# A two-layer trunk with attention and experts: routing by blocks in turn, four fold steps on VectorE, Q's weights between gate halves

## The chip, the cores and the metric

The kernel runs on one core of a Trainium2 chip. The metric is the device time of one execution in microseconds (us), as the median of several runs. 1216.5 us of the profiled execution are its span, from the first to the last instruction that the profile shows.

The core's engines work beside each other, each through its own list of instructions: TensorE (PE in the profile, PEld for its weight loads), VectorE (DVE), ScalarE (ACT), GpSimd (POOL) and SyncE (SP). SyncE does no arithmetic here; it issues the transfers of weights from the chip's memory, and where an issue has to wait, SyncE stands and everything behind that issue in its list waits too.

## The reference, cut to what matters

The model has two layers. Each has a token-mixing part and a part with experts, both steered by a vector c through six rows of "adaLN" (two shifts, two scales, two gates). There are 256 tokens of 1024 numbers, 32 experts of width 512 in 4 groups, and a token goes to two experts of one group.

```python
for l in range(DEPTH):
    mod = (jax.nn.silu(c) @ w_ada[l] + b_ada[l])[:, None, :]
    sh1, sc1, gt1, sh2, sc2, gt2 = jnp.split(mod, 6, axis=-1)
    h = x * (1 + sc1) + sh1
    proj = h @ w_in[l]
    q, k, v, u, vs = jnp.split(proj, split_at, axis=-1)
    att = diff_attention(rope(q), rope(k), v, lam)
    mix = concat(rms_norm(att), chunk_spatial_gate(u, vs)) @ w_out[l]
    x = layer_norm(DEEPNORM_ALPHA * x + (1 + gt1) * mix, ln1_g[l], ln1_b[l])
    h = x * (1 + sc2) + sh2
    ffn = hier_moe(h, w_grp, b_grp, w_rt, b_rt, w_gate, w_up, w_down)
    x = layer_norm(DEEPNORM_ALPHA * x + (1 + gt2) * ffn, ln2_g[l], ln2_b[l])
```

The parts `rope` and `concat` stand here for a few lines each.

## The kernel before

**The stream of weights.** 467.6 MB of weights are read, each once. Lines 81 to 149 write them into one list, `stream`, in the order in which they are to be loaded: for each layer the adaLN rows of the first part (`s1`), its gate (`g1`), the five sections of w_in (Q, K, V, U, VS), the adaLN rows of the second part (`s2`, eight chunks), w_out, the second gate (`g2`), then the experts. Most chunks are 1 MiB (128 partitions x 2048 numbers). They land in a ring of 18 slots of 1 MiB, which are nine pairs, `w0` to `w8` (the names w_78 to w_86 in the rows of order below). `choose` (line 180) takes one free slot, or for a chunk of 2 MiB a whole free pair. `pump` (line 193) issues the next chunks on SyncE's queue as long as slots are free, and `done` (line 230) gives a slot back once the program has written its last use, and pumps. So a chunk's transfer waits on the chip for the last reader of the chunk that held its slot.

**The experts.** They are sorted by use, so that experts without tokens come last, and are worked on in units (line 52): units 0 to 5 of two experts, with chunks of 1 MiB, and units 6 to 10 of four experts, with whole 2 MiB chunks for the gate, up and down matrices (in units 6 to 9). The order of the last two units is exchanged, so the experts without tokens fall into unit 9, and their loads and matmuls are skipped at run time. For each unit PE gathers tokens (`gps`), runs gate and up (L1297), then down (`dps`, L1387) and adds to `y` (L1306).

**The front of a layer.** `mixing` (line 644) runs the sections, the attention and the output projection `wo`. While PE does that, VectorE folds adaLN weights: `ada_fold` (line 511) is a generator, and each step multiplies 128x512 of a chunk by the matching part of silu(c) and adds it into chunk 0 (L520). A chunk takes four steps. `done` of a chunk stands behind its four steps, so it runs when the generator is asked for the step after them:

```python
        for k in range(4 if (l, part) == (0, "s2") else KD):
            ...
            if k:
                done(("ada", l, part, k))
```

`fold_on(n)` asks n times. `ada_sum` (line 455) then sums chunk 0 over the partitions with four matmuls (L459); chunks that weren't folded take four matmuls each with silu(c) (L464). `ada_cols` (line 497) copies that row with ScalarE, turns it into columns with PE (`adaT`), and copies these with VectorE into `modc`. In layer 0, four of the eight s2 chunks are folded and four are multiplied on PE, in the routing; in layer 1 all eight are folded, and the sum stands in `mixing`.

**The routing** (`routing`, line 1009). It takes X, normalised by `normalise(tci)` for each of the two blocks of 128 tokens (VectorE's statistics, ScalarE's Ln and Exp for the root, then VectorE), makes `hT` (transposes `hTps` on PE, then a scale and shift by `gc` and `bc`, on VectorE and ScalarE or, with `both=False`, on ScalarE alone), takes the logits (`rt`), chooses experts on VectorE, and splits X into three bf16 parts (`part`, `subtract`: a part is cast by ScalarE, PE subtracts it from X in `left`, and so on), which the gathers need. `gate_sum` for g2 (L539) runs in two halves of two chunks, `gate_copy` (L546) copies its row with ScalarE.

The program's order on each engine is the order in which the code calls these steps; there is no planner.

## Time and profile before

| | us |
|---|---|
| median of 3 runs (1219.26 to 1220.87) | 1219.34 |
| the profiled execution | 1218.11 |
| its span | 1216.5 |
| PE busy in the span | 1044.8 |
| VectorE busy | 356.4 |
| ScalarE busy | 157.0 |

The transfers moved 467.60 MB at a mean of 384 GB/s, and the mean granted clock of PE was 0.931 of its full speed. A busy engine alone says little here, since PE and the transfers take turns as the bound: the slices of the span (GB/s) say when the transfers are full, the timeline of SyncE says where an issue stands and for how long, and the timeline of PE, with the idle time ahead of a group in brackets and what ended it, says what PE was waiting for. A timeline row joins like instructions of a line that follow each other; its first number is the start in us from the start of the span, its second how long the group lasts. A matmul of four bytes stands as two records in the trace.

### The profile page before, as it was taken

Reading aid. Unit: us, or ns where it says so; the run is one execution under the profiler, and the core shown is the slowest. Engines: PE = TensorE matmul, PEld = TensorE weight load, DVE = VectorE, ACT = ScalarE, POOL = GpSimd, SP = SyncE. Lnnn points to the kernel's source line nnn. Section 1 sums busy time; section 2 is a strip of 40 time slices with the busy share of each in tenths; the row PEclk is TensorE's granted clock in tenths of the full one; section 3 lists DMA queues with packets and bytes.
Section 4 is the critical chain, followed back from the end, with each engine's and each line's share of the span. In section 5 each row is a group of like instructions: output and inputs, shape, how many; then the busy total and the mean of one; then the engine's idle time right before and its main releaser. Section 6 shows DMA issues by size and latency. Waiting matters only on the chain. (4 is left out here: it accounts for less than half of the span.)

```text
span 1216.5 us, 13939 instructions
## 1 busy us (share of the span) xinstructions
PE 1044.8 (86%) x5351; PEld 422.9 (35%) x5353; DVE 356.4 (29%) x845; ACT 157.0 (13%) x384; POOL 24.1 (2%) x35
## 2 busy tenths in 40 slices
PE   6999998999997767689789998899999868667785
PEld 2465453434342221133135654443434213113221
DVE  1386767112120010031148535621112101003103
ACT  2033132101010010000022323210101001000000
POOL 0200000000000000000000400000000000000000
PEclk8999999999998787799999998989999978788898
DMA  9999989899999999999999953789999999999995
GB/s 320 375 406 352 418 305 370 366 403 421 423 427 427 427 427 427 429 382 421 394 397 401 413 197 139 313 327 406 421 421 429 426 428 429 426 428 428 421 409 197
DMA packets 79963, 467.60 MB, mean 384 GB/s; under 512 B 11053, under 2 KB 11585, under 8 KB 43154
## 3 DMA queue, kind: packets, MB, share of 16 engines
q1 hardware_dynamic: 79522, 465.85, 94.3%
q8 instruction: 45, 0.74, 0.2%
q10 hardware_dynamic: 288, 0.52, 0.1%
q0 software_dynamic: 80, 0.26, 0.1%
q14 instruction: 28, 0.23, 0.0%
HBM read 484.44 MB, written 1.05 MB: 399 GB/s over the span
## 5 line engine op out<-in xcount | busy, mean ns | idle before, releaser
L1387 PE MATMUL dps<-w,eaT_moe 128*32 128x512 f32 (+1 forms) x1024 | 196.7, 668 | 46.4 <-DMA w<-in_w_down_dram 37.7
L1297 PE MATMUL up<-w,XT_moe 128*32 128x512 f32 (+1 forms) x1024 | 184.7, 644 | 38.3 <-DMA w<-in_w_up_dram 38.3
L1297 PE MATMUL gate<-w,XT_moe 128*32 128x512 f32 (+1 forms) x1024 | 184.4, 652 | 33.1 <-DMA w<-in_w_gate_dram 31.0
L1387 PEld LDWEIGHTS dps<-w,eaT_moe 128*32 128x32 f32 (+1 forms) x1024 | 52.5, 131 | 174.6 <-issue 110.8
L1297 PEld LDWEIGHTS gate<-w,XT_moe 128*32 128x32 f32 (+1 forms) x1024 | 53.1, 128 | 157.5 <-issue 107.0
L1353 DVE TENSOR_TENSOR act_moe<-sg_moe,up 128x512 f32<-128x512 f32 x22 | 15.1, 688 | 314.6 <-PE up L1297 285.6
L1297 PEld LDWEIGHTS up<-w,XT_moe 128*32 128x32 f32 (+1 forms) x1024 | 50.9, 127 | 161.8 <-issue 107.4
L1393 DVE TENSOR_TENSOR eo_moe<-dps,gt 128x512 f32<-128x512 f32 x44 | 30.4, 692 | 210.6 <-PE dps L1387 210.6
L650 PE MATMUL sec<-w,hT_front 128*128 128x512 f32 x192 | 84.8, 595 | 2.6 <-DMA w<-in_w_in_dram 2.4
L1306 PE MATMUL y<-eo_moe,wt_moe 128*128 128x512 f32 x176 | 84.9, 607 | 1.6 <-DVE eo_moe L1393 1.6
L1275 PE MATMUL gps<-G_moe,Xp_moe 128*128 128x256 bf16 (+1 forms) x672 | 64.5, 250 | 3.8 <-DVE G_moe L1249 1.5
L1343 ACT ACTIVATE sg_moe<-gate 128x512 f32<-128x512 f32 x22 | 13.1, 597 | 414.9 <-PE gate L1297 414.9
L1281 DVE TENSOR_SCALAR XT_moe<-gps,gc,bc 128x128 f32<-128x128 f32 x88 | 30.6, 405 | 123.0 <-PE gps L1275 123.0
L1275 PEld LDWEIGHTS <-Xp_moe 128*128 128x128 bf16 x672 | 53.1, 98 | 21.9 <-issue 13.0
L650 PEld LDWEIGHTS sec<-w,hT_front 128*128 128x128 f32 x192 | 35.5, 190 | 44.6 <-issue 39.6
L1306 PEld LDWEIGHTS y<-eo_moe,wt_moe 128*128 128x128 f32 x176 | 30.2, 191 | 43.6 <-issue 40.2
L1321 ACT COPY wt_moe<-wtps 128x256 f32<-128x256 f32 x22 | 8.2, 373 | 275.6 <-PE wtps L1319 275.6
L1284 ACT ACTIVATE XT_moe<-gps,bc,gc 128x128 f32<-128x128 f32 x88 | 33.8, 456 | 41.2 <-PE gps L1275 41.2
L520 DVE SCALAR_TENSOR_TENSOR w<-w,csl,w 128x512 f32<-128x512 f32 x56 | 39.1, 768 | 0.0
L659 PE MATMUL sec<-w,hT_front 128*128 128x512 f32 x64 | 30.1, 627 | 1.9 <-DVE hT_front L673 1.9
L842 PE MATMUL u<-hT_front,w 128*128 128x256 f32 x128 | 28.8, 379 | 0.0
L955 PE MATMUL wo<-w,zu_front 128*128 128x512 f32 x64 | 28.1, 592 | 0.0
(283 smaller groups left out, 755.4 us busy)
## 6 DMA issues: line engine op xcount, KB each, us to landing
w<-in_w_gate_dram SPq DMA_DIRECT2D x64, 1024.0 KB, 9.8
w<-in_w_up_dram SPq DMA_DIRECT2D x64, 1024.0 KB, 14.0
w<-in_w_gate_dram SPq DMA_DIRECT2D x32, 2048.0 KB, 24.5
w<-in_w_up_dram SPq DMA_DIRECT2D x32, 2048.0 KB, 22.9
w<-in_w_down_dram SPq DMA_DIRECT2D x32, 2048.0 KB, 23.3
w<-in_w_down_dram SPq DMA_DIRECT2D x56, 1024.0 KB, 13.6
w<-in_w_ada_dram SPq DMA_DIRECT2D x40, 1024.0 KB, 15.2
w<-in_w_in_dram SPq DMA_DIRECT2D x20, 1024.0 KB, 14.8
```

The costliest lines, as they stand in the source:

```text
L520: yield V.scalar_tensor_tensor(acc[:, c], w[:, c], csl[:, k:k + 1], acc[:, c], op0=ALU.mult, op1=ALU.add)
L650: T.matmul(ps, hT[:, k, tci * P:(tci + 1) * P], held["in", l, s, k // 4][:, k % 4, :], start=(k == 0), stop=(k == KD - 1))
L659: T.matmul(ps, hT[:, k, tci * P:(tci + 1) * P], held["in", 0, s, hf][:, k % 4, :], start=(k == 0), stop=(k == KD - 1))
L842: T.matmul(ps[:, 0:NT], held["in", l, U_, k // 4][:, k % 4, g * P:(g + 1) * P], hT[:, k, :], start=(k == 0), stop=(k == KD - 1))
L955: T.matmul(o_ps[tci][h], (cat, zu)[hf][:, kk, tci * P:(tci + 1) * P], w[:, kk, :], start=(hf == 1 and kk == 0), stop=(hf == 0 and kk == 3))
L1275: T.matmul(ps[:, k - kk].rearrange("p j s -> p (j s)"), parts[:, a, tci, k, :], g[:, tci, js[0] * P:(js[-1] + 1) * P], start=(a == 0 and t ...
L1281: V.tensor_scalar(dst, ps[:, k - kk, i, :], gc[:, k:k + 1], bc[:, k:k + 1], op0=ALU.mult, op1=ALU.add)
L1284: S.activation(dst, ps[:, k - kk, i, :], AF.Identity, scale=gc[:, k:k + 1], bias=bc[:, k:k + 1])
L1297: T.matmul(ps[c0:c0 + w], xt[:, k, c0:c0 + w], held[nm, l, place, part][:, k - part[0], :], start=(k == 0), stop=(k == KD - 1))
L1306: T.matmul(y[tci][h], wt[:, tci, :], eo[:, h, :], start=(i == 0), stop=(i == NU - 1))
L1387: T.matmul(dps[h][s0:s0 + w], aT[:, kk, s0:s0 + w], held["down", l, place, part][:, kk - ks[0], c0:c0 + 512], start=(kk == 0), stop=(kk == ...
L1393: V.tensor_tensor(eo[:, h, :], dps[h], gt2[:, h * 512:(h + 1) * 512], op=ALU.mult)
```

## The change

There are four parts.

1. *The folds of layer 0.* s2's chunks 4 to 7 are loaded ahead of w_out instead of behind it, and `ada_fold` folds all eight. In layer 0 the 12 requests in the U section go; 6 come behind the last scores, 6 behind the second block's attention, 4 behind the first residual. The sum of s2 and its columns move from the routing (layer 0) and from the first half of wo (layer 1) to between the last groups of wo.
2. *The routing, in both layers alike.* hT of block 0 is ScalarE's alone; the first half of g2's gate and the first subtraction stand behind it; `normalise(1)` moves from the end of `mixing` to behind that; block 1's transposes and `left` go to other PSUM pools; the parts of block 0 and 1 are cast and subtracted in another order; and the gate's second half and its copy stand ahead of the gathers in both layers (before, in layer 0 the second half stood in `experts`, and the copy in both).
3. *The start of layer 1.* Q's two chunks are loaded between the halves of g1, and the matmuls of Q's first block and the second block's transposes stand ahead of the second gate half. The last statistics of layer 0's second block move from the end of `experts` to behind hT of block 0.
4. `gr` instead of `gsum` is handed from `routing` to `experts` (not shown).

```diff
         if l > 0:
-            add_ada(l, "g1", range(4))
-            add_in(l, [Q_, K_, VS_])
+            add_ada(l, "g1", range(2))
+            add_in(l, [Q_])
+            add_ada(l, "g1", range(2, 4))
+            add_in(l, [K_, VS_])
         add_ada(l, "s2", range(4 if l == 0 else 8))
...
             add_ada(l + 1, "s1", range(4, 8))
+            add_ada(l, "s2", range(4, 8))
         add_out(l)
-        if l == 0:
-            add_ada(l, "s2", range(4, 8))
         add_ada(l, "g2", range(4))
...
         acc = held["ada", l, part, 0][:, 0, :]
-        for k in range(4 if (l, part) == (0, "s2") else KD):
+        for k in range(KD):
             w = held["ada", l, part, k][:, 0, :]
...
             make_hT(lambda k: hT[:, k], gc, bc, 0, early)
-            gate_sum(l, "g1", 2, gsum1)
+            V.bn_stats(sts[1][:, 1, :], y_prev[1][1])
             normalise_psum(1, y_prev[1], sts[1])
             q0 = section(l, Q_, 0)
+            make_hT(lambda k: hT[:, k], gc, bc, 1, early)
+            gate_sum(l, "g1", 2, gsum1)
             gr1 = gate_copy(l, 2, gsum1, fp, "gr")
-            make_hT(lambda k: hT[:, k], gc, bc, 1, early)
         else:
...
         rescale_part(2)
-        fold_on(12)
+        fold_on(12 if l else 0)
         u_part(3)
...
         S.copy(vv[:, 1, :], section(l, V_, 1))
+        if l == 0:
+            fold_on(6)
         ovs = [py.tile([P, 512], F32, tag="s", name=f"att{qc}").rearrange("t (h d) -> t h d", h=H) for qc in range(NTC)]
...
         fold_too(6)
-        asum2 = None
         for tci in range(NTC):
...
                 wo(tci, h, 1)
-            if l > 0 and tci == 0:
-                asum2 = ada_sum(l, "s2", KD)
-            elif l > 0:
-                ada_cols(l, 2, asum2, fp)
             att_T(tci, ats[tci])
             fold_too(8 if tci == 0 else 0)
+            fold_on(0 if tci == 0 else 6)
         ats.clear()
-        asum = None
+        asum = asum2 = None
         for tci in range(NTC):
...
                     ada_cols(l + 1, 0, asum, fp)
+                elif tci == 1 and h == 0:
+                    asum2 = ada_sum(l, "s2", KD)
+                elif tci == 1 and h == 1:
+                    ada_cols(l, 2, asum2, fp)
                 wo(tci, h, 0)
                 residual(tci, h, o_ps[tci][h], gt1, fp)
-            normalise(tci)
+                if tci == 0 and h == 0:
+                    fold_on(4)
+            if tci == 0:
+                normalise(0)
 
...
                 k = slice(4 * h, 4 * h + 4)
-                S.copy(parts[:, a, tci, k], left[tci][h].rearrange("t (k d) -> t k d", k=4))
-
-        def subtract(a, tci):
-            if a == 0:
-                left[tci] = [py.tile([P, 512], F32, tag="s", name=f"left{tci}{h}") for h in range(2)]
-            for h in range(2):
+                S.copy(parts[:, a, tci, k], left[tci, h].rearrange("t (k d) -> t k d", k=4))
+
+        def subtract(a, tci, hs=(0, 1)):
+            for h in hs:
                 k = slice(4 * h, 4 * h + 4)
                 if a == 0:
-                    T.matmul(left[tci][h], ident, X[:, tci, k, :], start=True, stop=False)
-                T.matmul(left[tci][h], minus, parts[:, a, tci, k], start=False, stop=True, skip_group_check=(a > 0))
+                    pool, tag = ((py, "s"), (pm, "m"))[tci]
+                    left[tci, h] = pool.tile([P, 512], F32, tag=tag, name=f"left{tci}{h}")
+                    T.matmul(left[tci, h], ident, X[:, tci, k, :], start=True, stop=False)
+                T.matmul(left[tci, h], minus, parts[:, a, tci, k], start=False, stop=True, skip_group_check=(a > 0))
 
...
         part(0, 0)
-        if l == 0:
-            asum2 = ada_sum(l, "s2", KD // 2)
-            ada_cols(l, 2, asum2, fp, py)
-            gc, bc = affine_cols(l, 1)
-            subtract(0, 0)
-            make_hT(hk, gc, bc, 0, early)
-            part(1, 0)
-        else:
-            gc, bc = affine_cols(l, 1)
-            make_hT(hk, gc, bc, 0, early, both=False)
-            subtract(0, 0)
-            gsum = gate_sum(l, "g2", 5)
-            part(1, 0)
+        gc, bc = affine_cols(l, 1)
+        make_hT(hk, gc, bc, 0, early, both=False)
+        gsum = gate_sum(l, "g2", 5)
+        subtract(0, 0)
+        normalise(1)
         for kk in (0, 4):
-            early[1, kk] = transpose_X(pm, "m", 1, kk)
+            early[1, kk] = transpose_X(py, "s", 1, kk)
         make_hT(hk, gc, bc, 1, early)
         part(0, 1)
+        part(1, 0)
         logits(0)
-        subtract(1, 0)
         logits(1)
...
         subtract(0, 1)
+        subtract(1, 0)
+        part(1, 1)
         part(2, 0)
-        part(1, 1)
-        if l == 0:
-            gsum = gate_sum(l, "g2", 5)
-        else:
-            gate_sum(l, "g2", 5, gsum)
+        gate_sum(l, "g2", 5, gsum)
         subtract(1, 1)
         part(2, 1)
+        gr = gate_copy(l, 5, gsum, fp)
         gl = lg[:, :, 0:NG]
...
         gather(0, (0,))
-        if l == 0:
-            gate_sum(l, "g2", 5, gsum)
-        gr = gate_copy(l, 5, gsum, mp)
         comb, pc = rest(mp)
...
             scatter(NU - 1, tci, (1,))
-            V.bn_stats(st[:, tci, 1, :], y[tci][1])
+            if tci == 0 or l + 1 == L:
+                V.bn_stats(st[:, tci, 1, :], y[tci][1])
         sts = [st[:, tci] for tci in range(NTC)]
```

On PE, from layer 0's last attention matmuls to the routing, the order of before reads as follows (`ada_s` with `onec` is a sum of folded chunks, with `csl` the product with silu(c); `wo` with `cg` are the last four groups of the output projection):

```order
L459 MATMUL ada_s_925<-w_79,onec 32x512 x4
L955 MATMUL wo_882<-w_78,cg_front_773 128x512 x4
L504 MATMUL adaT<-ident,adar_0_front_938 64x128 x8
L955 MATMUL wo_887<-w_79,cg_front_773 128x512 x4
L955 MATMUL wo_907<-w_78,cg_front_773 128x512 x4
L955 MATMUL wo_913<-w_79,cg_front_773 128x512 x4
L629 MATMUL hTps<-ident,X 128x128 x8
L459 MATMUL ada_s_1030<-w_85,onec 32x512 x4
L464 MATMUL ada_s_1030<-w_81,csl 32x512 x4
L464 MATMUL ada_s_1030<-w_82,csl 32x512 x8
L464 MATMUL ada_s_1030<-w_80,csl 32x512 x4
L504 MATMUL adaT<-ident,adar_2_moe_1056 64x128 x8
```

and the order of the changed kernel, at the same place:

```order
L460 MATMUL ada_s_939<-w_79,onec 32x512 x4
L959 MATMUL wo_889<-w_78,cg_front_780 128x512 x4
L505 MATMUL adaT<-ident,adar_0_front_957 64x128 x8
L959 MATMUL wo_894<-w_82,cg_front_780 128x512 x4
L460 MATMUL ada_s_998<-w_85,onec 32x512 x4
L959 MATMUL wo_914<-w_78,cg_front_780 128x512 x4
L505 MATMUL adaT<-ident,adar_2_front_1012 64x128 x8
L959 MATMUL wo_920<-w_82,cg_front_780 128x512 x4
L630 MATMUL hTps<-ident,X 128x128 x8
L437 LDWEIGHTS pick_137
L437 MATMUL gate_g_1071<-rw_136,pick_137 32x512
L437 LDWEIGHTS pick_137
```

The s2 sum (`ada_s_1030` before, `ada_s_998` now) has lost its products with `csl`, and it and its `adaT` have moved ahead of hTps, between wo groups; behind hTps stands the gate's first half.

On SyncE, the loads that follow layer 1's s1 chunks were, before (w_78 to w_86 are the nine pairs; a row with x2 stands for two loads):

```order
L223 DMA w_86<-in_w_out_dram 128x4x512
L223 DMA w_78<-in_w_out_dram 128x4x512 x2
L223 DMA w_79<-in_w_out_dram 128x4x512
L223 DMA w_81<-in_w_ada_dram 128x2048
L223 DMA w_82<-in_w_ada_dram 128x2048 x2
L223 DMA w_80<-in_w_ada_dram 128x2048
L223 DMA w_83<-in_w_ada_dram 128x2x1024 x2
L223 DMA w_80<-in_w_ada_dram 128x2x1024
L223 DMA w_81<-in_w_ada_dram 128x2x1024
```

and are now:

```order
L224 DMA w_78<-in_w_ada_dram 128x2048 x2
L224 DMA w_79<-in_w_ada_dram 128x2048
L224 DMA w_81<-in_w_ada_dram 128x2048
L224 DMA w_82<-in_w_out_dram 128x4x512
L224 DMA w_86<-in_w_out_dram 128x4x512
L224 DMA w_78<-in_w_out_dram 128x4x512
L224 DMA w_82<-in_w_out_dram 128x4x512
L224 DMA w_80<-in_w_ada_dram 128x2x1024
L224 DMA w_83<-in_w_ada_dram 128x2x1024 x2
```

The four 128x2048 loads of w_ada behind the s1 chunks are s2's 4 to 7: they have moved ahead of the four of w_out, into the pairs w_78, w_79 and, the last, w_81.

On PE, at the start of layer 1 (`gate_g` is g1's gate, `sec_0_0` and `sec_0_1` are Q of the two blocks), the order of before:

```order
L436 MATMUL gate_g_3828<-rw_136,pick_137 32x512
L436 LDWEIGHTS pick_137
L436 MATMUL gate_g_3828<-rw_136,pick_137 32x512
L539 MATMUL gate_g_3828<-w_80,csl 32x512 x8
L629 MATMUL hTps<-ident,X 128x128 x8
L539 MATMUL gate_g_3828<-w_84,csl 32x512 x8
L650 MATMUL sec_0_0_3901<-w_86,hT_front_3827 128x512 x8
L629 MATMUL hTps<-ident,X 128x128 x8
L650 MATMUL sec_0_1_3932<-w_86,hT_front_3827 128x512 x8
```

and of the changed kernel:

```order
L437 MATMUL gate_g_3826<-rw_136,pick_137 32x512
L437 LDWEIGHTS pick_137
L437 MATMUL gate_g_3826<-rw_136,pick_137 32x512
L540 MATMUL gate_g_3826<-w_83,csl 32x512 x8
L630 MATMUL hTps<-ident,X 128x128 x8
L651 MATMUL sec_0_0_3890<-w_85,hT_front_3825 128x512 x8
L630 MATMUL hTps<-ident,X 128x128 x8
L540 MATMUL gate_g_3826<-w_84,csl 32x512 x8
L651 MATMUL sec_0_1_3931<-w_85,hT_front_3825 128x512 x8
```

Q of block 0 and the second transposes have moved ahead of the gate's second half.

## Rows read from the trace of the kernel before

**Rows 1.** Page: GB/s moved in 40 slices of 30.4 us.

```profile
GB/s 320 375 406 352 418 305 370 366 403 421 423 427 427 427 427 427 429 382 421 394 397 401 413 197 139 313 327 406 421 421 429 426 428 429 426 428 428 421 409 197
```

**Rows 2.** Windows: span, busy us by engine (x instructions), PEclk, DMA share, GB/s.

```profile
212.00:217.00 5.00, 5.00 (x22) 1.67 (x20) 0.77 (x1) 0.00 (x0) 0.00 (x0) 0.86 0.24 59
250.00:530.00 280.00, 230.38 (x1222) 78.71 (x1222) 39.55 (x74) 15.83 (x38) 0.00 (x0) 0.90 1.01 425
530.00:535.00 5.00, 5.00 (x48) 1.46 (x44) 0.64 (x1) 0.00 (x0) 0.00 (x0) 0.92 0.85 364
535.00:540.00 5.00, 4.85 (x72) 3.15 (x68) 1.46 (x4) 2.21 (x5) 0.00 (x0) 1.00 0.70 242
792.00:799.00 7.00, 6.80 (x22) 2.35 (x24) 2.92 (x4) 0.00 (x0) 0.00 (x0) 0.64 0.16 66
```

**Rows 3.** Timeline of SyncE, layer 0: start, duration, line, operation, count.

```profile
199.67 16.71 SPq L223 DMA_DIRECT2D w<-in_w_gate_dram  x4
...
523.25 13.98 SPq L223 DMA_DIRECT2D w<-in_w_down_dram  x4
```

**Rows 4.** Timeline of PE, layer 0's routing; in brackets idle time before, and releaser.

```profile
158.13 1.06 PE L459 MATMUL ada_s<-w,onec 128*32 128x512 f32 x8
159.01 3.62 PE L464 MATMUL ada_s<-w,csl 128*32 128x512 f32 x32
163.33 1.09 PE L504 MATMUL adaT<-ident,adar_moe 128*64 128x128 f32 x8 [0.71 <-ACT adar_moe L499]
...
172.28 1.93 PE L1029 MATMUL left<-X,ident 128*128 128x512 f32 x2
...
185.68 0.65 PE L1297 MATMUL gate<-w,XT_moe 128*64 128x512 f32 x2 [0.76 <-ACT gr_moe L546]
```

**Rows 5.** Timeline of VectorE, layer 0's attention and output projection.

```profile
122.34 1.02 DVE L800 COPY aT_front<-aTps 128x384 f32<-128x384 f32 x2 [4.12 <-PE aTps L798]
123.28 1.41 DVE L520 SCALAR_TENSOR_TENSOR w<-w,csl,w 128x512 f32<-128x512 f32 x2
...
146.18 0.69 DVE L987 TENSOR_TENSOR res_front<-wo,cg_front 128x512 f32<-128x512 f32 x1 [4.11 <-PE wo L955]
...
150.49 0.69 DVE L987 TENSOR_TENSOR res_front<-wo,cg_front 128x512 f32<-128x512 f32 x1 [1.66 <-PE wo L955]
```

**Rows 6.** SyncE's waits from 520 to 540: total us, times, longest.

```profile
SPq L223 <- PE gate L1297: 12.2, 1, 12.2
```

**Rows 7.** Timeline of PE, unit 9 of layer 0.

```profile
527.20 8.77 PE L1297 MATMUL gate<-w,XT_moe 128*32 128x512 f32 x64
```

**Rows 8.** Timeline of PE, where layer 1 begins.

```profile
614.81 1.09 PE L629 MATMUL hTps<-ident,X 128*128 128x128 f32 x8 [1.59 <-ACT X L621]
615.83 2.23 PE L539 MATMUL gate_g<-w,csl 128*32 128x512 f32 x16
620.45 7.10 PE L650 MATMUL sec<-w,hT_front 128*128 128x512 f32 x16 [2.39 <-DMA w<-in_w_in_dram]
...
628.59 1.95 PE L650 MATMUL sec<-w,hT_front 128*128 128x512 f32 x4 [0.16 <-DVE hT_front L639]
```

**Rows 9.** Timeline of PE, layer 1's routing.

```profile
741.30 1.02 PE L1029 MATMUL left<-X,ident 128*128 128x512 f32 x2
745.88 0.61 PE L1030 MATMUL left<-Xp_moe,minus 128*128 128x512 bf16 x1 [3.55 <-ACT Xp_moe L1017]
...
758.04 1.76 PE L1029 MATMUL left<-X,ident 128*128 128x512 f32 x2
...
767.90 1.51 PE L1297 MATMUL gate<-w,XT_moe 128*64 128x512 f32 x6 [1.38 <-ACT gr_moe L546]
```

**Rows 10.** Timeline of ScalarE, layer 1's routing.

```profile
747.03 2.90 ACT L641 ACTIVATE hT_moe<-hTps,bc,gc 128x128 f32<-128x128 f32 x8 [1.21 <-DVE gc L576]
```

**Rows 11.** Timeline of VectorE, layer 1's routing.

```profile
745.56 0.81 DVE L614 TENSOR_SCALAR X<-X,mv,rs 128x1024 f32<-128x1024 f32 x1
```

**Rows 12.** Timeline of SyncE, unit 9 of layer 1.

```profile
1106.86 14.32 SPq L223 DMA_DIRECT2D w<-in_w_down_dram  x4
```

8 lines of the change are left out of this document (4 added, 4 removed).

## The prediction

> **What bounds the kernel now.** I read the page's slices first. GB/s says where the weights set the time: at 421 and more the transfers are the bound, and where it falls to 305, 352 or 139 they are not [rows 1]. The windows then put times on the falls. Through layer 0's experts from 250 to 530 us DMA is full at 425 GB/s; at 212 to 217 it moves 59 GB/s while PE is busy all the time, and at 792 to 799, the same place of layer 1, 66 GB/s [rows 2]. There SyncE stands before an issue: four loads that it began at 199.67 took 16.71 us to issue [rows 3]. It waits because the ring of 18 slots is full and PE has not yet used up a chunk. So in a front PE's pace sets when a slot comes free, and in the experts DMA sets the pace. The end moves with the last stall of DMA in each layer: a microsecond saved on PE ahead of 247 or of 799 us is a microsecond at the end, and a chunk that the ring can hold less is the time of a chunk at the end. A chunk of 1 MiB (1.049 MB) at 425 GB/s takes 2.5 us and one of 2 MiB 4.9 us.
>
> There is one more hole, at 530 to 540 us, with 364 and then 242 GB/s [rows 2]. It is unit 9 of layer 0 (of 0 to 10), which skips two of its four experts. SyncE issues that unit's first down chunk at 523.25 and can't issue the second until PE is through with gate [rows 3]: it waits 12.2 us for it [rows 6], and gate runs from 527.20 for 8.77 us, to 535.97 [rows 7]. What had been issued lasts until some 534 us (364 of 425 GB/s are 4.3 us of the five from 530).
>
> **Layer 0's routing.** PE's L464 matmuls of s2 go: 3.62 us [rows 4]. The eight matmuls left (1.06 us) and adaT (1.09 us) move between the wo groups, at the same cost to PE, but the wait of 0.71 us for ScalarE's copy ahead of adaT is then hidden by a wo group. The gate row's copy now stands ahead of the gathers on ScalarE, so the 0.76 us before gate(0) go [rows 4]. Together 5.1 us less. Against it stands one new wait. With `both=False` all eight activations of hT(0) are ScalarE's, and normalise(1), which stood ahead of them, now needs ScalarE's Ln and Exp behind them. In layer 1, where the trace has the same eight, they take 2.90 us [rows 10], and X(1) was ready at 745.56 + 0.81 = 746.37 [rows 11]. By my replay of the order (an estimate), gc and bc stand at 743.2, the eight end at 746.1, and Ln, Exp and what follows of the normalisation, 1.9 us, end near 748.0, 1.6 us later than before. PE, which has half of g2's gate and a left pair ahead of X(1)'s transposes now, comes there at 746.5 to 747.2. So PE waits between nothing and all of the 2.9 us; I take 1.2, the middle of 0.8 and 1.5 from the replay. Layer 0: -5.1 + 1.2 = **-3.9 us** (from -5.1 to -2.2).
>
> The 16 matmuls become 16 VectorE steps. Two of them take 1.41 us [rows 5], so 16 cost 11.3 us of VectorE. Twelve stand in front of a wait: six fill the 4.12 us before the aT copy at 122.34, six the 4.11 us before the residual at 146.18 (6 x 0.705 = 4.2 us each) [rows 5]. The last four (2.8 us) stand behind the first residual, ahead of the next at 150.49, which had 1.66 us to wait: it starts 1.1 us later [rows 5]. The later residuals' products come 1 to 2 us later too, since PE has 2.15 us more between its wo groups, so VectorE has caught up by the last. I cost the folds at nothing; without that cover it would be 1.2 us. Their chunks now come ahead of w_out, which pushes w_out by 4 MiB, 9.9 us; as PE's first wo comes after the attention, I expect no wait there.
>
> **The ring.** Folding frees a chunk when its generator is asked for one step more: `done` of chunk k runs on the way to the first step of chunk k + 1, and for chunk 7 only on a 33rd request. Layer 0 now asks 8 + 8 + 6 + 6 + 4 = 32 times. So `done(("ada", 0, "s2", 7))` is never reached, and in the order of SyncE's issues that slot, the second half of w_81, is given to nobody after it: no whole pair of 2 MiB is ever put in w_81 again. From there the ring has 17 slots, and for loads of 2 MiB eight pairs instead of nine. Layer 1 asks for 41, so nothing is lost there a second time. That has three prices. In each layer's front, where DMA runs dry waiting for a slot [rows 2, 3], chunk n waits for the release of n - 17 instead of n - 18: one chunk later, **+2.5 us** in layer 0 and **+2.5 us** in layer 1. If the ring were not what limits, this would be 0 each; if a pair were lost where a pair is needed, 4.9. In unit 9 the chunk that kept DMA busy to the last, until 534 (down 28, 2 MiB, issued at 523.25) finds no pair, and has to wait for gate's end at 535.97 as the ones behind it do. DMA runs dry one 2 MiB chunk earlier and starts again at the same time: **+4.9 us** (0 if something else frees a pair in time; no more, since the restart is set by PE). Elsewhere in the units of four PE is through with a chunk 7 to 10 us after its landing, and eight pairs last 39 us; no hole opens there.
>
> For these three prices the Trainium skill ("DMA: Bandwidth & Descriptors", section Bandwidth) would name another rate: for transfers from HBM the HBM side, some 358 GB/s, is said to bind. By that 1 MiB would take 2.9 us and the three together 11.7 us instead of 9.9. The trace differs with its 425 GB/s.
>
> **Layer 1's front.** Q is 2 MiB nearer, so its chunks land 4.9 us sooner, and Q0 stands ahead of the second gate half. Before, PE had that half at 615.83 and then waited 2.39 us for Q's weights until 620.45 [rows 8]. Now Q0 can start when hT(0) is there: the transposes end at 614.81 + 1.09 = 615.9, the first slice 0.4 later, 616.3. 7.1 us of Q0, the transposes of the second block and the gate half (some 3.0 us together) put Q1 at 626.4, against 628.59 [rows 8]: **-2.2 us** (from -3.0, without the 0.4 and with Q there first, to -1.2, if half of Q's lead is lost on the way). K and U come no later than they did; s2 lands ahead of its folds or about with them.
>
> **Layer 1's routing.** The wait of 3.55 us for the cast of X(0), which stood behind normalise(1) on ScalarE, goes, and the 1.38 us before gate(0) go: -4.9. The same new wait of 1.2 comes: **-3.7 us** (from -4.9 to -2.0) [rows 9].
>
> **The sum.** -3.9 + 2.5 + 4.9 - 2.2 - 3.7 + 2.5 = +0.1 us. On the profiled execution (span 1216.5, with 1.6 us around it 1218.1) that gives 1218.2; the median of the runs shown lies 1.2 above it. I predict 1219.4. Less than 0.2% (2.4 us) from no change can't be told by a measurement of this kernel. The forecast's own range, from the middle parts of the bounds above, is 1217 to 1221.8.
>
> **Rivals.**
> 1. The lost slot costs little: the issues ahead of a stall rearrange, or DMA makes up for unit 9. Then -9.8 remains of the gains alone: 1219.3 - 9.8 = 1209.5. For it: nothing in PE's own work grows. Against it: three stalls with SyncE standing before an issue [rows 2, 3, 6]. Decides: whether DMA restarts at the hole of unit 9 before gate's end. 18%.
> 2. PE's clock. After the wait of 3.55 us two left matmuls take near double: five such pairs stand in the two routings, from 1.93 us at 172.28 [rows 4] to 1.76 at 758.04, against 1.02 for the same pair at 741.30, ahead of the wait [rows 9]; 1.02 is the 2.4 GHz level, the others are at 1.2 GHz for most of it. If with fewer waits the clock stays up, five times 0.8 us more go: 1219.4 - 4.0 = 1215.4. The Trainium skill ("TensorE: Matmul & The Clock Gate", Part 1, What's actually happening) has the half clock as the default that activity lifts, which speaks for this; the rows agree with their 1.02 and 1.93. Against it: a wait of PE for X(1) remains. 15%.
> 3. Layer 1 gets a hole of its own. Its unit 9 skips one expert; SyncE began its down issues at 1106.86 and took 14.32 us over four [rows 12], with the DMA slices around it at 428 GB/s [rows 1]. With one pair less what is issued lasts, by a replay of the issues, to about 2 us beyond gate's end. If gate ends over 2 us later against the transfers, DMA stops, for up to 4.9 us: 1219.4 + 4 = 1223.4, slower. 14%.
> 4. Routing gains less: the wait for X(1) is 2.9 us in both layers instead of 1.2: 1219.4 + 3.4 = 1222.8, slower. 15%.
>
> **Chances.** The forecast has 38%, of which nothing lies outside 0.2%. Faster by over 0.2%: rivals 1 and 2, 0.33. Slower: rivals 3 and 4, 0.29. Same: 0.38. The range 1210 to 1224.5 leaves out half of rival 1 and the upper part of 3 and 4.
>
> **What would show it.** In the changed profile: gate(0) of layer 0 some 3.9 us earlier than 185.68, but the fall of GB/s after it no shorter; the hole at 530 to 540 wider by one 2 MiB chunk, with SyncE waiting for gate from one issue earlier; Q1 2.2 us earlier against the end of layer 0's experts; gate(0) of layer 1 5.9 us earlier against the same end; layer 1's units without a hole. Gate(0) earlier and the end earlier by as much would make the forecast wrong on the ring; gate(0) no earlier would make it wrong on the routing.

## The result, and the profile after

| | before | changed |
|---|---|---|
| median, us | 1219.3 (10 runs, 1216.0 to 1223.9) | 1224.7 (10 runs, 1223.3 to 1230.0) |
| ratio to before | | 1.0051, 95% interval 1.0035 to 1.0068 |
| span of the profiled execution, us | 1216.5 | 1226.9 |
| mean granted clock of PE | 0.931 | 0.920 |

The changed kernel is slower, by 5.4 us in the medians and 6.2 by the ratio. I had forecast 1219.4 us, no change, with a range up to 1224.5. The profiled execution of the changed kernel took 1228.6 us and is one of its slower ones, so its rows show some 4 us more than the median has.

The slices of the page (GB/s moved, 40 slices of 30.7 us), against [rows 1]:

```profile
GB/s 319 374 407 305 412 336 340 336 403 420 421 429 427 429 427 429 426 295 419 400 392 409 405 192 201 298 325 402 421 421 427 424 428 427 428 427 429 421 410 205
```

In the fronts the slices differ both ways; the eighteenth, with unit 9 of layer 0, has fallen from 382 to 295. Set side by side at equal bytes moved, the two traces say where the time went: the changed kernel is 6.4 us late from 100 MB on, when layer 0's fours begin; 12.9 us late behind unit 9; and 10.9 us late from 310 MB to the end, so layer 1's front gave 2 us back. Three places, then.

**Layer 0's routing.** PE's timeline of the changed kernel, as [rows 4] (start, us, and in brackets the idle time ahead and what ended it):

```profile
169.48 1.15 PE L630 MATMUL hTps<-ident,X 128*128 128x128 f32 x8 [2.45 <-DVE X L615]
...
170.50 3.61 PE L1052 MATMUL rt<-wr,hT_moe 128*128 128x36 f32 x16
...
173.97 3.61 PE L1052 MATMUL rt<-wr,hT_moe 128*128 128x36 f32 x16
177.38 2.05 PE L1036 MATMUL left<-X,ident 128*128 128x512 f32 x2
...
188.26 4.08 PE L1295 MATMUL gate<-w,XT_moe 128*64 128x512 f32 x18
```

PE waits 2.45 us for X(1) ahead of the second transposes, where I had put 1.2. And then it runs slowly: the 32 records of logits (two blocks of 16) take 3.61 us a block, where before they took 1.95, and the first pair of left 2.05. The granted clock of that stretch is the first of these windows of the changed kernel (span, busy us of PE, PEld, DVE, ACT, POOL, then PEclk, DMA share, GB/s), the others are unit 9:

```profile
169.50:177.50 8.00, 8.00 (x43) 7.97 (x43) 1.37 (x4) 3.41 (x7) 0.00 (x0) 0.55 1.00 416
525.00:531.00 6.00, 5.30 (x40) 1.18 (x32) 2.06 (x3) 0.00 (x0) 0.00 (x0) 0.97 0.42 126
531.00:540.00 9.00, 6.54 (x34) 1.64 (x38) 6.83 (x8) 0.00 (x0) 0.00 (x0) 0.62 0.99 421
540.00:546.00 6.00, 5.85 (x71) 2.79 (x64) 0.73 (x2) 1.27 (x3) 0.00 (x0) 1.00 0.28 74
```

A PEclk of 0.55 means that PE was at its lower level, 1.2 GHz, for nearly all of 169.5 to 177.5. The wait itself is what ScalarE makes VectorE wait, in its timeline and VectorE's:

```profile
164.72 2.89 ACT L642 ACTIVATE hT_moe<-hTps,bc,gc 128x128 f32<-128x128 f32 x8
167.47 0.23 ACT L585 ACTIVATE rsy<-rsv 128x1 f32<-128x1 f32 x1
```

```profile
165.63 0.15 DVE L583 TENSOR_SCALAR rsv<-mv 128x1 f32<-128x1 f32 x1
167.97 0.22 DVE L591 SCALAR_TENSOR_TENSOR rst<-rsy,rsv 128x1 f32<-128x1 f32 x1 [2.19 <-ACT rsy L586]
```

VectorE had the variance of block 1 at 165.8. ScalarE's Ln and Exp came behind all eight activations of hT(0), at 167.5, so VectorE stood idle for 2.19 us, ahead of the few steps that end in X(1). Gate(0) began at 188.26, against 185.68 in [rows 4].

**Unit 9.** SyncE's timeline of the changed kernel, as [rows 3]:

```profile
508.76 5.52 SPq L224 DMA_DIRECT2D w<-in_w_gate_dram  x4
528.81 1.96 SPq L224 DMA_DIRECT2D w<-in_w_up_dram  x4
543.87 1.97 SPq L224 DMA_DIRECT2D w<-in_w_down_dram  x4
```

The last gate load was issued by 514.3 us, and the first up load at 528.8; the windows above show DMA at 126 GB/s from 525 to 531, full again from 531 to 540, and at 74 GB/s from 540 to 546. So there are two holes, of 4.2 us (6 us x (1 - 126/425)) and 5.0 us, where before there was one of some 3 us [rows 2].

**Layer 1.** Q0 began right behind the first transposes, with no wait (before: 2.39 us [rows 8]):

```profile
627.17 1.09 PE L630 MATMUL hTps<-ident,X 128*128 128x128 f32 x8 [0.87 <-ACT X L622]
628.33 7.13 PE L651 MATMUL sec<-w,hT_front 128*128 128x512 f32 x16
...
638.72 5.82 PE L651 MATMUL sec<-w,hT_front 128*128 128x512 f32 x13 [0.53 <-DVE ropeb_front L716]
```

and in the routing the same wait came, with part of the same slow stretch behind it; gate(0) had no wait ahead of it any more [rows 9]:

```profile
758.37 1.09 PE L630 MATMUL hTps<-ident,X 128*128 128x128 f32 x8 [2.46 <-DVE X L615]
...
759.33 2.19 PE L1052 MATMUL rt<-wr,hT_moe 128*128 128x36 f32 x16
...
761.39 3.61 PE L1052 MATMUL rt<-wr,hT_moe 128*128 128x36 f32 x16
...
775.52 7.09 PE L1295 MATMUL gate<-w,XT_moe 128*64 128x512 f32 x32
```

### The profile page after: what moved, and what is told of

The parts are those of the page before. It is cut to its first block, busy times and chain, and to the rows that moved or that the text cites. A ratio compares the mean times of both kernels' runs of the same rounds, so it can differ in the third digit from the quotient of the medians.

```text
span 1226.9 us, 13888 instructions
## 1 busy us (share of the span) xinstructions
PE 1056.6 (86%) x5321; PEld 426.6 (35%) x5321; DVE 364.9 (30%) x857; ACT 157.9 (13%) x388; POOL 23.8 (2%) x35
## 4 chain that ended last, share of the span: by engine, by line
PE 31%; DMA 17%; DVE 2%; SPq 1%; issue 1%; ACT 1%; DVEq 0%; ACTq 0%
DMA w<-in_w_down_dram 8%; DMA w<-in_w_up_dram 6%; PE dps L1382 5%; PE gate L1295 5%; PE up L1295 5%; PE sec L651 5%; DMA w<-in_w_gate_dram 3%; PE wo L959 2%; PE y L1304 2%; PE gps L1273 1%; SPq L224 1%; PE u L844 1%; PE y L1311 1%; PE rt L1052 0%; DVE XT_moe L1279 0%
## 5 line engine op out<-in xcount | busy, mean ns | idle before, releaser
L1295 PE MATMUL up<-w,XT_moe 128*32 128x512 f32 (+1 forms) x1024 | 196.0, 671 | 45.4 <-DMA w<-in_w_up_dram 45.3
L1388 DVE TENSOR_TENSOR eo_moe<-dps,gt 128x512 f32<-128x512 f32 x44 | 30.4, 691 | 200.4 <-PE dps L1382 200.4
L1338 ACT ACTIVATE sg_moe<-gate 128x512 f32<-128x512 f32 x22 | 13.1, 597 | 415.4 <-PE gate L1295 415.4
L521 DVE SCALAR_TENSOR_TENSOR w<-w,csl,w 128x512 f32<-128x512 f32 x76 | 52.6, 760 | 0.7 <-issue 0.7
L660 PE MATMUL sec<-w,hT_front 128*128 128x512 f32 x64 | 30.4, 631 | 1.9 <-DVE hT_front L674 1.9
L959 PE MATMUL wo<-w,cg_front 128*128 128x512 f32 x64 | 28.9, 597 | 0.0
## 6 DMA issues: line engine op xcount, KB each, us to landing
w<-in_w_gate_dram SPq DMA_DIRECT2D x64, 1024.0 KB, 12.9
```

The costliest lines, as they stand in the source:

```text
L521: yield V.scalar_tensor_tensor(acc[:, c], w[:, c], csl[:, k:k + 1], acc[:, c], op0=ALU.mult, op1=ALU.add)
L660: T.matmul(ps, hT[:, k, tci * P:(tci + 1) * P], held["in", 0, s, hf][:, k % 4, :], start=(k == 0), stop=(k == KD - 1))
L959: T.matmul(o_ps[tci][h], (cat, zu)[hf][:, kk, tci * P:(tci + 1) * P], w[:, kk, :], start=(hf == 1 and kk == 0), stop=(hf == 0 and kk == 3))
L1295: T.matmul(ps[c0:c0 + w], xt[:, k, c0:c0 + w], held[nm, l, place, part][:, k - part[0], :], start=(k == 0), stop=(k == KD - 1))
L1388: V.tensor_tensor(eo[:, h, :], dps[h], gt2[:, h * 512:(h + 1) * 512], op=ALU.mult)
```

## The experiments

Each kernel below was run beside the kernel before, whose median was 1218.2 to 1218.6 us in these comparisons (1219.3 beside the changed kernel). A ratio is to that kernel. Where kernels of different comparisons are set against each other, the ratios are the safer measure. The names are the runs' labels: "released" means that the lost slot is given back.

| run | median, us | runs | ratio, 95% interval |
|---|---|---|---|
| changed kernel | 1224.7 | 10 | 1.0051 (1.0035 to 1.0068) |
| f1_release | 1218.4 | 13 | 1.0005 (0.9993 to 1.0018) |
| l1_before_lost_slot | 1228.8 | 6 | 1.0086 (1.0065 to 1.0107) |
| n1_old_routing | 1212.9 | 12 | 0.9966 (0.9949 to 0.9984) |
| q1_old_q_order | 1221.5 | 12 | 1.0023 (1.0008 to 1.0038) |
| q2_q_order_alone | 1213.0 | 6 | 0.9952 (0.9935 to 0.9969) |
| d1_folds_alone | 1218.2 | 11 | 1.0000 (0.9986 to 1.0013) |
| f5_gate_in_the_wait | 1207.7 | 6 | 0.9909 (0.9894 to 0.9925) |
| f2_normalise_earlier | 1207.5 | 6 | 0.9913 (0.9891 to 0.9935) |
| f6_both | 1205.4 | 5 | 0.9890 (0.9874 to 0.9907) |
| f7_gate_behind_the_wait | 1214.3 | 11 | 0.9964 (0.9947 to 0.9981) |
| l6_both_lost_slot | 1213.4 | 12 | 0.9966 (0.9950 to 0.9983) |
| q6_both_old_q_order | 1208.8 | 6 | 0.9917 (0.9898 to 0.9935) |

After the result there were two theories. A: the lost slot of the ring makes it slower. B: the new routing does. They are not exclusive, so the first four runs undo one part each.

### The slot: f1_release and l1_before_lost_slot

```diff
                 if tci == 0 and h == 0:
-                    fold_on(4)
+                    fold_on(5)
```

> The changed kernel with one request more to the fold generator in layer 0 (5 instead of 4 behind the first residual), so that s2's last chunk gives its slot back and nine pairs are there again. Nothing else differs. Theory A (the lost slot is what made it slower): by the two profiles it cost 2.5 us in each front and 6.5 us at unit 9 of layer 0, 11.5 us in all, so this kernel takes some 1213 us, 0.5% under the kernel before, and the transfers of unit 9 of layer 0 stop only once, as before. Rival B (the routing is what made it slower: the new wait of 2.45 us for X(1) in each layer, and PE's lower clock behind it): the slot costs 3 us or less, and this kernel takes 1221 us or more, still slower than before.

Measured: 1218.4 us, 6.3 less than the changed kernel (its ratio is 0.0046 lower, 5.6 us), between the two outcomes. So both theories are half right: giving the slot back doesn't make the kernel faster than before, but takes away what it was slower by. Most of the hole at unit 9 goes; the first window is layer 0's logits, the second the hole:

```profile
169.00:176.00 7.00, 7.00 (x36) 7.00 (x34) 0.93 (x3) 3.41 (x7) 0.00 (x0) 0.50 1.02 424
530.00:540.00 10.00, 9.85 (x116) 4.73 (x112) 4.28 (x7) 1.87 (x5) 0.00 (x0) 1.00 0.95 387
```

387 GB/s in the second is less of a hole than before had (303 over the same ten us, from [rows 2]). In the first, the granted clock is 0.50 here too.

```diff
                          start=(k == 0), stop=(k == KD - 1))
-            done(("ada", l, part, k))
+            if (l, part, k) != (0, "s2", KD - 1):
+                done(("ada", l, part, k))
```

> The kernel before, in which the slot of layer 0's last s2 chunk is never given back (its release is left out; no arithmetic changes). So the lost slot alone, with the routing and the folds as before. Theory A: 11.5 us more, 1231 us (+0.9%), with a hole of DMA at unit 9 of layer 0 that is some 6.5 us longer. My prediction's sum would have given 9.9 us. Rival B: 3 us more or less.

Measured: 1228.8 us, 10.3 more than the kernel before, with nothing else changed. Its SyncE at unit 9:

```profile
505.87 5.51 SPq L223 DMA_DIRECT2D w<-in_w_gate_dram  x4
525.92 1.96 SPq L223 DMA_DIRECT2D w<-in_w_up_dram  x4
540.94 1.96 SPq L223 DMA_DIRECT2D w<-in_w_down_dram  x4
```

As in the changed kernel, up's loads start only at 525.9, 14.5 us after the last of gate. In the traces, set side by side at equal bytes, this kernel is 3.5 us late ahead of unit 9, 9.9 behind it and some 12 us late at the end: the three places that I had named, with 6.4 us at unit 9 in place of 4.9.

### The routing: n1_old_routing

```diff
-            if tci == 0:
-                normalise(0)
+            normalise(tci)
...
-        gc, bc = affine_cols(l, 1)
-        make_hT(hk, gc, bc, 0, early, both=False)
-        gsum = gate_sum(l, "g2", 5)
-        subtract(0, 0)
-        normalise(1)
+        if l == 0:
+            gc, bc = affine_cols(l, 1)
+            subtract(0, 0)
+            make_hT(hk, gc, bc, 0, early)
+            part(1, 0)
+        else:
+            gc, bc = affine_cols(l, 1)
+            make_hT(hk, gc, bc, 0, early, both=False)
+            subtract(0, 0)
+            gsum = gate_sum(l, "g2", 5)
+            part(1, 0)
...
```

What follows in `routing`, and the gate's second half and copy, are as in the kernel before too.

> The released kernel (all eight chunks folded, Q's weights between the gate halves) with the routing's order of the kernel before in each layer, except that the s2 sum stays where the change put it. Against f1_release this is the new routing alone. If the prediction's steps hold, the new routing is worth 0 us in layer 0 beyond the matmuls that left it and 3.7 us in layer 1, so this kernel takes some 3.5 us more than f1_release. If the wait for X(1) and the lower clock eat it, as the profile of the changed kernel suggests (gate(0) of layer 0 came 1.6 us later against wo's begin instead of earlier), this kernel takes no longer than f1_release, or up to 3 us less.

Measured: 1212.9 us, 5.5 less than f1_release (4.8 by the ratios), beyond what the second outcome of the expectation had allowed for. q1_old_q_order and d1_folds_alone, below, are the same pair with Q in its old place: there the new routing costs 3.3 us. So the new routing, meant to shorten the way to gate(0), costs 3.3 to 5.5 us. That is theory B, and somewhat less than the slot.

The traces show only part of it. From the first transposes (hTps) to gate(0), layer 0 takes 24.9 us in n1 and 26.7 in f1_release, but layer 1 takes 27.1 us in n1 and 21.7 in f1_release's profiled execution, the fastest of its 13 at 1211.3 us (26.7 in q1's, which lies at its median). A trace of f1_release near its median is not there. What is on record for every run is the mean granted clock of PE: its median is 0.924 over f1_release's runs and 0.9345 over n1's.

### Why the routing costs: f5, f2, f6, f7

Theory C: the wait for X(1) is paid twice, once itself and once since PE's granted clock falls behind it. Rival D: the logits are slow because nothing parts their 32 small matmuls any more. f5 fills the wait with work (the diffs of f5, f2, f6 and f7 are against f1_release):

```diff
         subtract(0, 0)
         normalise(1)
+        gate_sum(l, "g2", 5, gsum)
...
         part(2, 0)
-        gate_sum(l, "g2", 5, gsum)
```

> The released kernel (f1_release) with the second half of g2's gate, 1.9 us of PE, right behind the first subtraction, where PE waits 2.46 us for X(1). No other engine's order changes. Theory C (the wait is paid twice: once itself, and once because PE's granted clock falls to the half level behind it and the 32 logits matmuls then take 3.61 us per block instead of 1.95): with PE busy up to X(1) the wait is some 0.5 us, rt takes 1.95 us per block in both layers in every profile, and in each layer 1.9 us of gate leave the way behind the logits: up to 5 us a layer less than f1_release, in all 6 to 10 us, 1209 to 1212 us. Rival D (the logits run slow because they are 32 small matmuls in a row, no longer parted by a subtraction): rt stays at 3.61, only the filled wait is gained, 1.9 us a layer, 1214.5 us.

Measured: 1207.7 us, 10.7 less than f1_release, a little more than C had allowed. PE in layer 0's routing:

```profile
167.94 1.09 PE L630 MATMUL hTps<-ident,X 128*128 128x128 f32 x8 [0.61 <-DVE X L615]
...
168.90 1.95 PE L1052 MATMUL rt<-wr,hT_moe 128*128 128x36 f32 x16
...
170.72 2.18 PE L1052 MATMUL rt<-wr,hT_moe 128*128 128x36 f32 x16
```

The wait is 0.61 us, and the logits, as bare of subtractions as in f1_release, take 1.95 and 2.18 us. So D as it was put, with the logits at 3.61 us and 1214.5 us in all, falls. Part of it is left: in the second block the clock fell after all, and the left pair behind it took 2.06 us, with PE busy all the time from the transposes on.

f2 shortens the wait without touching PE's order:

```diff
-        make_hT(hk, gc, bc, 0, early, both=False)
+        make_hT(hk, gc, bc, 0, early, both=False, between=lambda: normalise(1))
         gsum = gate_sum(l, "g2", 5)
         subtract(0, 0)
-        normalise(1)
...
         for kk in range(0, KD, 4):
+            if kk and between:
+                between()
```

> The released kernel with normalise(1) between the first four and the last four of ScalarE's activations of hT(0), instead of behind all eight. So X(1) comes some 1.4 us earlier and PE's wait for it falls from 2.46 to about 1.0 us. Theory C: with the shorter wait the clock stays up in most executions; 3 to 6 us less than f1_release, 1212 to 1215. Rival D: 1.4 us a layer, 1215.6, with rt at 3.61 as before.

Measured: 1207.5 us, 10.9 less, more than expected. In its profiled execution (1207.8 us) layer 0's wait is down to 1.06 us, but the clock still fell, in the logits:

```profile
166.86 1.09 PE L630 MATMUL hTps<-ident,X 128*128 128x128 f32 x8 [1.06 <-DVE X L615]
...
167.81 2.35 PE L1054 MATMUL rt<-wr,hT_moe 128*128 128x36 f32 x16
...
170.03 3.61 PE L1054 MATMUL rt<-wr,hT_moe 128*128 128x36 f32 x16
```

```profile
168.00:174.00 6.00, 6.00 (x34) 5.92 (x34) 1.28 (x6) 3.40 (x7) 0.00 (x0) 0.60 1.01 421
```

and in layer 1, behind 1.08 us, it didn't: 1.95 us a block. So with a wait of about a microsecond the clock falls in some places or executions and not in others. Two places in one execution can't say how often, nor that it was the wait that brought the clock down.

f6 does both.

```diff
-        make_hT(hk, gc, bc, 0, early, both=False)
+        make_hT(hk, gc, bc, 0, early, both=False, between=lambda: normalise(1))
         gsum = gate_sum(l, "g2", 5)
         subtract(0, 0)
-        normalise(1)
+        gate_sum(l, "g2", 5, gsum)
...
         part(2, 0)
-        gate_sum(l, "g2", 5, gsum)
```

> f2_normalise_earlier and f5_gate_in_the_wait together: the gate's second half ahead of X(1)'s transposes and normalise(1) between the halves of hT(0)'s activations. X(1) is there before PE is through with the gate, so PE doesn't wait at all. Theory C: as f5 or up to 1 us a layer better, 1208 to 1211 us, the fastest of all. Rival D: 1213.

Measured: 1205.4 us, 1.1% faster than the kernel before, below the expected range and the lowest median of all, though the intervals of f5 and f2 overlap with its own. Its profiled execution, at 1201.3, is the fastest of its runs. In it there is no wait and the clock stays full, gate(0) at 180.42 against 185.68 in [rows 4]:

```profile
165.92 1.92 PE L540 MATMUL gate_g<-w,csl 128*32 128x512 f32 x16
167.77 1.10 PE L630 MATMUL hTps<-ident,X 128*128 128x128 f32 x8
...
168.73 1.95 PE L1054 MATMUL rt<-wr,hT_moe 128*128 128x36 f32 x16
...
170.55 1.95 PE L1054 MATMUL rt<-wr,hT_moe 128*128 128x36 f32 x16
...
180.42 7.09 PE L1296 MATMUL gate<-w,XT_moe 128*64 128x512 f32 x32
```

That isn't so in every execution. l6_both_lost_slot and q6_both_old_q_order, below, have the same routing, and PE doesn't wait ahead of the logits in them either. In l6's layer 0 the logits were at full clock and left behind them was not:

```profile
170.05 1.95 PE L1054 MATMUL rt<-wr,hT_moe 128*128 128x36 f32 x16
171.84 1.66 PE L1038 MATMUL left<-X,ident 128*128 128x512 f32 x2
...
173.72 1.92 PE L1038 MATMUL left<-X,ident 128*128 128x512 f32 x2
```

At full clock such a pair takes 1.02 us. From 172 to 176 us PE was busy all the time, and the granted clock was 0.57. The same happened in both layers of q6's profile, but in neither of f6's and not in l6's layer 1. So behind the logits the clock can fall without any wait. In f1_release's layer 0, with the wait of 2.46 us ahead, it fell earlier, and the logits themselves ran at half clock.

f7 leaves the wait as it is and puts the gate's second half between it and the logits:

```diff
             early[1, kk] = transpose_X(py, "s", 1, kk)
+        gate_sum(l, "g2", 5, gsum)
...
         part(2, 0)
-        gate_sum(l, "g2", 5, gsum)
```

> The released kernel (f1_release) with the second half of g2's gate behind the transposes of X(1), ahead of the logits: the wait of 2.46 us for X(1) stays as it is, but behind it PE first has 1.9 us of matmuls of 512 columns instead of the 32 small ones of 36. If the wait alone sets how long the half clock lasts, the gate and part of the logits run at half clock, and nothing is gained but a place: 1217 to 1219 us. If what comes behind the wait sets how soon the clock is back (as in the kernel before, where left was slow behind a wait of 3.55 us and the logits were at full clock again), rt takes 1.95 us per block: 1212 to 1215 us.

Measured: 1214.3 us, 4.1 less than f1_release, inside the second outcome's range.

```profile
168.34 1.21 PE L630 MATMUL hTps<-ident,X 128*128 128x128 f32 x8 [2.46 <-DVE X L615]
169.48 3.44 PE L540 MATMUL gate_g<-w,csl 128*32 128x512 f32 x16
...
172.89 1.95 PE L1052 MATMUL rt<-wr,hT_moe 128*128 128x36 f32 x16
...
174.71 2.44 PE L1052 MATMUL rt<-wr,hT_moe 128*128 128x36 f32 x16
```

The same 2.46 us of wait, and the clock falls here as well: the gate takes 3.44 us instead of 1.92. But the logits behind it are at full clock again, until the clock falls a second time in their second block, and the left pair behind that is slow:

```profile
176.96 2.05 PE L1036 MATMUL left<-X,ident 128*128 128x512 f32 x2
```

In f1_release the logits were slow for all of their 7 us. So what stands behind the wait bore on which matmuls ran slow. That layer 0's routing gets shorter by it, these traces don't show: from hTps to gate(0) it takes 26.7 us in both. Where f7's 4.1 us come from stays open.

### The other parts: q1, q2, q6 and d1

```diff
-            add_ada(l, "g1", range(2))
-            add_in(l, [Q_])
-            add_ada(l, "g1", range(2, 4))
-            add_in(l, [K_, VS_])
+            add_ada(l, "g1", range(4))
+            add_in(l, [Q_, K_, VS_])
...
-            V.bn_stats(sts[1][:, 1, :], y_prev[1][1])
+            gate_sum(l, "g1", 2, gsum1)
             normalise_psum(1, y_prev[1], sts[1])
             q0 = section(l, Q_, 0)
-            make_hT(lambda k: hT[:, k], gc, bc, 1, early)
-            gate_sum(l, "g1", 2, gsum1)
             gr1 = gate_copy(l, 2, gsum1, fp, "gr")
+            make_hT(lambda k: hT[:, k], gc, bc, 1, early)
```

This edit makes q1 from f1_release and q6 from f6_both; q2 is its reverse on the kernel before.

> The released kernel with g1's four chunks ahead of Q's, the second gate half ahead of Q's first block, and the statistics of layer 0's last block where they were before. Against f1_release this is Q's new place alone. The prediction has 2.2 us for it (3.0 to 1.2): this kernel takes that much longer than f1_release, with an idle time of PE of some 2.4 us for Q's weights. Rival: Q's gain is given back later in layer 1's front, by s2 or the sections that come later, and the two are the same within 0.5 us.

> The kernel before with Q's weights between the gate halves alone (and the second gate half behind Q's first block, and the last statistics behind hT of block 0). The prediction has 2.2 us for it; between q1 and f1 it was 3.0 us. If the gain doesn't hang on the rest, this kernel is 2 to 3 us faster than the kernel before. If it does (since with the old routing the front of layer 1 has other waits), under 1 us.

> f6_both with g1's chunks ahead of Q's and the old order at layer 1's start: Q's new place alone once more, where the routing behind it no longer scatters. The prediction has 2.2 us, the two pairs so far 3.0 (q1 against f1) and 5.2 (q2 against the kernel before): this kernel takes 2 to 5 us more than f6_both, 1207.5 to 1210.5.

Measured: Q's new place is worth 3.0 us (q1 against f1_release), 5.2 (q2 against before, more than expected) and 3.4 (q6 against f6_both). In q2's profile Q0 starts at 615.23 and Q1 at 625.79, 2.8 us ahead of [rows 8]:

```profile
615.23 7.13 PE L652 MATMUL sec<-w,hT_front 128*128 128x512 f32 x16
...
625.79 7.13 PE L652 MATMUL sec<-w,hT_front 128*128 128x512 f32 x16 [0.70 <-ACT gr_front L548]
```

Some 0.7 us of it lie ahead of Q: with the new order, which also moves the last statistics, PE waits 0.87 us ahead of block 0's transposes (in q2 and in the changed kernel) instead of 1.59. And in q1's profile, with the old order, one reason shows why Q's place can be worth more than the wait:

```profile
623.45 10.17 PE L649 MATMUL sec<-w,hT_front 128*128 128x512 f32 x16 [2.37 <-DMA w<-in_w_in_dram]
```

Behind the wait of 2.37 us for Q's weights, Q0's 16 records took 10.17 us in place of 7.10. In l1's profile, also with the old order, they took 8.80 us; in those of the kernel before, d1 and q6 it did not happen. In the profiles of the changed kernel and of q2, with the new order, there is no such wait, and Q0 took 7.13 us.

```diff
-        for k in range(4 if (l, part) == (0, "s2") else KD):
+        for k in range(KD):
...
-        fold_on(12)
+        fold_on(12 if l else 0)
...
+                if tci == 0 and h == 0:
+                    fold_on(5)
...
-            asum2 = ada_sum(l, "s2", KD // 2)
-            ada_cols(l, 2, asum2, fp, py)
```

(and the moves of the s2 chunks, of the s2 sum and its columns, as in the change.)

> The kernel before with layer 0's folds alone (s2's chunks 4 to 7 ahead of w_out, all folded, the slot released; the s2 sum and its columns between wo's last groups in both layers); routing and layer 1's Q as before. The prediction takes 3.6 + 0.7 us out of layer 0's routing for it and nothing for VectorE: 4.3 us less than the kernel before. From n1_old_routing less q2_q_order_alone it would be nothing, from n1 less the 3.0 us of Q between q1 and f1 some 2.6.

Measured: nothing gained, 1218.2 us. The 3.62 us of matmuls are gone, but PE waits:

```profile
164.98 0.59 PE L1033 MATMUL left<-Xp_moe,minus 128*128 128x512 bf16 x1 [3.40 <-ACT Xp_moe L1020]
165.36 1.91 PE L1032 MATMUL left<-X,ident 128*128 128x512 f32 x2
...
168.74 1.51 PE L1048 MATMUL rt<-wr,hT_moe 128*128 128x36 f32 x12
```

In the order of the kernel before these matmuls had stood over the wait for the cast of X(0), which on ScalarE comes behind normalise(1). With them gone it shows as 3.40 us, as it did in layer 1 all along [rows 9], and left behind it is slow. So in the old routing the folds turn work into a wait. What they are worth in the new routing without its wait was not tried.

### The slot once more: l6_both_lost_slot

```diff
                 if tci == 0 and h == 0:
-                    fold_on(5)
+                    fold_on(4)
```

This is f6_both with the slot lost again.

> f6_both with 4 requests instead of 5 behind the first residual, so that the slot is lost again as in the changed kernel. With the new routing free of its wait, this is the lost slot alone a second time. Theory A: the slot costs the same whatever the routing, about 10 us as on the kernel before (1218.6 to 1228.8): 1215.5 us. Rival: only the 6.2 us that lay between the changed kernel and f1_release: 1211.6 us.

Measured: 1213.4 us, 8.0 more than f6_both, between the two outcomes. The slot has cost 10.3, 8.0 and 6.3 us in its three pairs. By their ratios to the kernel before they are 0.0086, 0.0076 and 0.0046, each with an interval of some 0.002 either way; one price of about 8 us lies within all three, only just. Whether the changed kernel's is really smaller stays open.

## Why the prediction was wrong, point by point

**The sum.** I had -3.9 + 2.5 + 4.9 - 2.2 - 3.7 + 2.5 = +0.1. The runs, put together one after the other, have: folds and Q together -5.6 (n1; alone 0 in d1 and -5.2 in q2), the new routing +5.5 (n1 to f1), the slot +6.3 (f1 to the changed kernel): +6.2. The slot I had at 9.9, so there I was too high, if anything. Where it failed is the routing; by the prediction's own sign, gate(0) of layer 0 was no earlier.

**The routing: the step that failed.** For the two routings with the folds I had -3.9 - 3.7 = -7.6 us; the runs have 0 + 5.5. Two steps failed: the wait for X(1) was too small, and the clock behind it stood in the sum at nothing.

The wait was in the prediction, with its reason (Ln and Exp behind hT(0)'s eight activations), but at 1.2 us, the middle of a replay; it was 2.45 and 2.46, nearer to the bound of 2.9 that the sum had. That is 2.5 us over both layers. The replay had X(1) nearly right, 7.6 us behind the start of hTps where it measured 7.9. But it let PE come there 6.1 to 6.8 us behind that start, and PE came after 5.4.

The rest is PE's clock. My own sum put a new wait in front of the logits, and rival 4 priced that wait at its own length. Behind it, in layer 0, the two blocks of logits took 3.61 us each instead of 1.95, which is 3.3 us. In the profiled execution these two terms make up what the two routings missed. From hTps to gate(0) layer 0 took 28.5 us before; less the 2.15 us that moved and the 5.1 that were to go, plus 1.2, the sum made it 22.5, and it took 26.7: 4.2 us more, 1.25 of them wait and about 3 clock. Layer 1 took 27.5 us before, the sum made it 23.7, and it took 25.0: 1.3 us more, which is the wait alone. Its granted clock was about what it had been: 0.86 over the 25.0 us, 0.88 over the 27.5 before. These 5.5 us are less than half of the 13.1 between -7.6 and +5.5; the rest no trace shows.

Rival 2 misread the rows that it was built on. Of its five slow pairs only one, at 746.28, stands right behind the wait of 3.55 us. The other four stand behind the logits, and in layer 0 no wait over 0.8 us stands ahead of them:

```profile
746.28 1.91 PE L1029 MATMUL left<-X,ident 128*128 128x512 f32 x2
```

```profile
170.00:172.50 2.50, 2.50 (x22) 2.26 (x22) 0.01 (x1) 1.83 (x3) 0.00 (x0) 0.99 1.02 429
172.50:175.00 2.50, 2.50 (x4) 0.96 (x4) 2.40 (x16) 0.33 (x1) 0.00 (x0) 0.50 0.71 301
```

So the kernel before already showed that the clock can fall behind the logits while PE is busy, and fewer waits alone could not promise that it stays up. The sentence from the Trainium skill ("TensorE: Matmul & The Clock Gate", Part 1, What's actually happening) that the half clock is the default and activity lifts it agrees with these traces only in part: 0.55 behind the wait of 2.45 us and 1.00 in f6_both with none, but 0.50 here with PE busy throughout. Nor is the fall certain. In layer 1 of f1_release's profiled execution the same wait stands, and the logits run at full clock; that execution was 7 us faster than the median:

```profile
746.08 1.09 PE L630 MATMUL hTps<-ident,X 128*128 128x128 f32 x8 [2.46 <-DVE X L615]
...
747.03 1.95 PE L1052 MATMUL rt<-wr,hT_moe 128*128 128x36 f32 x16
```

What the runs do show is the price of the wait with all that hangs on it: 10.7 us when it is filled (f5), 10.9 when it is shortened (f2). How much of that is the clock in a typical execution stays open.

**The folds.** "At nothing" for VectorE held: in the changed kernel the twelve steps filled the waits, the last four were made up by the last residual, which again waits for PE (1.03 us). But the gain that I booked for PE's 3.62 us is no gain by itself (d1), since these matmuls covered another wait. In the sum I had removed work and the idle times seen before, and asked only at X(1) what is late next.

**The ring.** That the slot is lost, that it costs a chunk in each front and a 2 MiB chunk or more at unit 9, held: l1 shows it with nothing else changed. (For layer 0's front I had 2.5 us. At 100 MB the changed kernel is 4.8 us behind f1_release, l1 2.9 behind the kernel before, and l6 1.5 behind f6.) The term for unit 9 was too small, 6.4 to 6.5 instead of 4.9: I followed the down chunk, but up's first chunk also finds no pair and waits for the unit before (528.8 instead of 507.3), and what is queued does not last that long; that two of the unit's four gate loads are skipped is the likely reason. Rival 1 (the slot costs little) is refuted. Rival 3 (a hole in layer 1's unit 9) didn't come: the changed kernel moves 425 GB/s from 1110 to 1150.

**Q.** -2.2 was 3 to 5 us. The step itself held: Q1 starts 11.55 us behind the first transposes in the changed kernel, against 13.78 before [rows 8], 2.2 less. Missing were the 0.7 us by which those transposes come sooner, and what a wait can do to the clock behind it (q1).

**The range.** The measured median lies 0.2 us above it. Rival 4 was the way it went, but I had it at the length of its wait, 1222.8. With the half clock of layer 0's logits added (3.3 us) it would have stood at 1226, beyond 1224.5. That the clock could fall in a routing was there to see, in [rows 4] and [rows 9].

## What to carry to other kernels

When a reorder puts a wait in front of small matmuls, price the wait and the stretch behind it at half clock, and put independent matmuls into the wait (10.7 us here; right behind it, 4.1). Before blaming a wait for a slow stretch, read the granted clock and the idle times ahead of it: here it also fell with no wait. When work is taken off an engine, ask which wait it was covering; the folds alone were worth nothing here. When a generator gives a resource back between two steps, count the requests: one `next` too few cost 6 to 10 us and made no other sign than eight names where there had been nine.
